# A sum of squares taken on VectorE and by products with ones, with the rotary angles moved behind it, in a two-layer hybrid transformer on one core

## The chip, the core and the metric

The kernel runs on one core of a Trainium2 chip. The metric is the device time of one execution in microseconds. The engines of the core are named as in the profile: PE (TensorE, the products), PEld (its weight loads), DVE (VectorE), ACT (ScalarE), POOL (GpSimd) and SP (SyncE, which here only issues DMAs).

## The reference

Two layers over 512 positions of width 1024, in float32. What matters here is the start of the first layer: the first norm, the rotary angles, and the first products that use both.

```python
def rmsnorm(x, g):
    xf = x.astype(jnp.float32)
    y = xf * lax.rsqrt(jnp.mean(xf * xf, axis=-1, keepdims=True) + EPS) * g.astype(jnp.float32)
    return y.astype(x.dtype)

def rope_tables(positions):
    inv_freq = ROPE_THETA ** (-jnp.arange(0, ROPE_DIM, 2, dtype=jnp.float32) / ROPE_DIM)
    ang = positions.astype(jnp.float32)[..., None] * inv_freq
    return jnp.cos(ang), jnp.sin(ang)

def reference(x, positions, ...):
    cos, sin = rope_tables(positions)
    for layer in range(DEPTH):
        h = rmsnorm(x, attn_norm[layer])
        if layer % 2 == 0:
            proj = h @ w_in_even[i]
            fq, fk, fv, ff, dq, ckv, dkr, iq, ik, iw = jnp.split(proj, split_points, axis=-1)
            ...   # forgetting attention, top-128 selected latent attention
        else:
            ...   # block attention
        x = x + conv_glu_ffn(rmsnorm(x, ffn_norm[layer]), ...)
    return rmsnorm(x, final_norm)
```

## The kernel before

x lies transposed: 8 tiles (d = 0 to 7) of 128 features by 512 positions. The norm is not applied ahead of the products. `prep` makes x times the gain, split in a high part xh (ACT, L169) and a low part xl (DVE, L170), and each product of a projection is three matmuls (L154 wh·xh, L155 wh·xl, L156 wl·xh). The factor 1/rms of each position is multiplied in later, as a row RB of 128 partitions by 512. Weights come in chunks of 128x1024 that ACT casts to a high part wh (L143; L126 for the first) and DVE or POOL turns into a low part wl (L149, L127; L147 on POOL). There are three buffers for each of raw, wh and wl, so a new chunk waits until an older one has been used.

The first layer starts with the projections misc, iq0, iq1 and ckv, 24 matmuls of 512 columns each. The norm's factor is found in `rstd_of`: the squares of the eight tiles (ACT) are added into one tile `acc`; four transposes (L187) put positions on partitions, DVE sums along the row (L189), a Newton iteration of small dependent DVE steps on 128x4 numbers (L190 to L196) gives y = 1/rms, and four more transposes (L199) spread y out as bc, which ACT copies to RB (L206). The rotary angles take a chain of some twenty small DVE steps (L285 to L305), one sine on ACT (L306, with a load of its table), and eight transposes (tabT, L321) that ACT copies to CT and ST. CR = CT·RB and SR = ST·RB (L212, L213) are what every rotated projection waits for.

The order of instructions on each engine is not the order in the source. A scheduler lays the whole program out on its own estimates and by the order of the source, then each engine runs its list strictly in order, with semaphores for what is late. So a change at the start can change places further on.

Of the kernel before, what the change touches and what calls it, by code (L numbers as in the profile page):

```python
# [18 lines left out]
F32 = mybir.dt.float32  # L19
F32R = mybir.dt.float32r  # L20
I32 = mybir.dt.int32
AF = mybir.ActivationFunctionType
OP = mybir.AluOpType
PSUM = bass.MemoryType.PSUM

P = 128
T = 512
NB = T // P
D = 1024
KT = D // P  # L30
# [41 lines left out]
def hybrid_kernel(ctx: ExitStack, tc: tile.TileContext, xT_d, pos_d, const_d, vec_d, w_d, out_d, idx):  # L72
    nc = tc.nc
    V, A, G, PE = nc.vector, nc.scalar, nc.gpsimd, nc.tensor
# [4 lines left out]
    tp = ctx.enter_context(tc.tile_pool(name="tp", bufs=1))  # L79
# [8 lines left out]
    def tmp(name):  # L88
        return tp.tile([P, T], F32, tag="tmp", name=name, bufs=N_TMP)

    def col(name, n=1):
        return tp.tile([P, n], F32, tag=f"col{n}", name=name, bufs=N_COL)

    def ps(tag, name, shape=(P, T)):
        return pp.tile(list(shape), F32, tag=tag, name=name, bufs=N_PSUM[tag])
# [5 lines left out]
    xT = cp.tile([P, KT, T], F32, name="xT")  # L101
# [5 lines left out]
    V.memset(table, 0.0)  # L107
    A.copy(table, table)
    ident = const[:, C_ID:C_ID + P]
    cmask = cp.tile([P, T], F32, name="cmask")  # L110
    G.memset(cmask[:, :384], 0.0)
    selr = cp.tile([P, P + 8], F32R, name="selr")
# [18 lines left out]
    def chunk(name, cut=0):  # L131
        raw = wp.tile([P, 1024], F32, tag="raw", bufs=N_W, name=f"raw_{name}")
        wh = wp.tile([P, 1024], F32R, tag="wh", bufs=N_W, name=f"wh_{name}")
        wl = wp.tile([P, 1024], F32R, tag="wl", bufs=N_W, name=f"wl_{name}")
        if cut:
            for s in (slice(0, cut), slice(cut, 1024)):
                nc.sync.dma_start(raw[:, s], w_d[idx[name]][:, s])
                split(wh[:, s], wl[:, s], raw[:, s])
                if s.start == 0:
                    nc.sync.dma_start(xT[:, 1], xT_d[:, 1])  # L140
            return wh, wl
        nc.sync.dma_start(raw, w_d[idx[name]])
        A.copy(wh, raw)  # L143
        if lo_on_pool:
            for n in range(0, 1024, 256):
                t = slice(n, n + 256)
                G.tensor_tensor(wl[:, t], raw[:, t], wh[:, t].bitcast(F32), op=OP.subtract)  # L147
        else:
            V.tensor_tensor(wl, raw, wh.bitcast(F32), op=OP.subtract)  # L149
        return wh, wl  # L150

    def mm3(out, ah, al, bh, bl, first, last):

        PE.matmul(out, ah, bh, start=first, stop=False)  # L154
        PE.matmul(out, ah, bl, start=False, stop=False)  # L155
        PE.matmul(out, al, bh, start=False, stop=last)  # L156

    def proj(name, w=None):
        wh, wl = w or chunk(name)
        o = ps("mm", f"mm_{name}")  # L160
        for k in range(KT):
            s = slice(k * P, k * P + P)
            mm3(o, wh[:, s], wl[:, s], xh[:, k], xl[:, k], k == 0, k == KT - 1)
        return o

    def prep(d, g, acc):

        gc = vec[:, V_G + 8 * g + d:V_G + 8 * g + d + 1]
        A.activation(xh[:, d], xT[:, d], AF.Identity, scale=gc)  # L169
        V.scalar_tensor_tensor(xl[:, d], xT[:, d], gc, xh[:, d].bitcast(F32), op0=OP.mult, op1=OP.subtract)  # L170
        if acc is not None:
            square(d, acc)

    def square(d, acc):

        if d == 0:
            A.activation(acc, xT[:, 0], AF.Square)
        else:
            s = tmp(f"sq{d}")
            A.activation(s, xT[:, d], AF.Square)  # L180
            (V if d == KT - 1 else G).tensor_tensor(acc, acc, s, op=OP.add)

    def rstd_of(acc, n, nm, nb=NB):

        st = ps("T", f"st_{nm}")[:, :nb * P]
        for b in range(nb):
            PE.transpose(st[:, b * P:b * P + P], acc[:, b * P:b * P + P], ident)  # L187
        ms, y, h, t = (col(f"{c}_{nm}", nb) for c in ("ms", "y", "h", "t"))
        V.reduce_sum(ms, st.rearrange("p (b c) -> p b c", b=nb), axis=mybir.AxisListType.X)  # L189
        V.tensor_scalar(ms, ms, 1.0 / n, EPS, op0=OP.mult, op1=OP.add)  # L190
        V.tensor_scalar(t.bitcast(I32), ms.bitcast(I32), 1, None, op0=OP.logical_shift_right)
        V.tensor_scalar(y.bitcast(I32), t.bitcast(I32), -1, 0x5F3759DF, op0=OP.mult, op1=OP.add)
        for _ in range(3):
            V.scalar_tensor_tensor(h, y, -0.5, y, op0=OP.mult, op1=OP.mult)
            V.tensor_tensor(h, h, ms, op=OP.mult)
            V.scalar_tensor_tensor(y, h, 1.5, y, op0=OP.add, op1=OP.mult)  # L196
        bc = ps("T", f"bc_{nm}")[:, :nb * P]
        for b in range(nb):
            PE.transpose(bc[:, b * P:b * P + P], y[:, b:b + 1].to_broadcast([P, P]), ident)  # L199
        return y, bc  # L200

    scale = {}

    def rstd_main(acc, nm):
        y, bc = rstd_of(acc, D, nm)
        A.copy(RB, bc)  # L206
        r = cp.tile([P, NB], F32, name=f"rstd_{nm}")
        V.tensor_copy(r, y)
        scale["col"] = r

    def rope_scaled():
        V.tensor_tensor(CR, CT, RB, op=OP.mult)  # L212
        V.tensor_tensor(SR, ST, RB, op=OP.mult)  # L213
# [12 lines left out]
    def scaled(o, nm):  # L226
        y = tmp(f"sc_{nm}")
        V.tensor_tensor(y, o, RB, op=OP.mult)
        return y
# [37 lines left out]
    def rope_angles():  # L267

        def fl(t):
            return t.rearrange("p b f -> p (b f)")  # L270

        def ang_tile(nm, k=1):
            return cp.tile([P, k * NB, 8], F32, name=f"ang_{nm}")

        def rnd(nm, src, k, c=1):
            t = ang_tile(nm, c)
            V.tensor_scalar(fl(t), fl(src), k, MAGIC, op0=OP.mult, op1=OP.add)
            V.tensor_scalar(fl(t), fl(t), -MAGIC, None, op0=OP.add)
            return t

        def fma(dst, a, k, b):
            V.scalar_tensor_tensor(fl(dst), fl(a), k, fl(b), op0=OP.mult, op1=OP.add)

        pf = cp.tile([P, NB, 1], F32, name="posf")
        V.tensor_copy(pf, pos)  # L285
        ang = ang_tile("x")
        freq = vec[:, V_FREQ:V_FREQ + 8].rearrange("p (b f) -> p b f", b=1)
        V.tensor_tensor(ang, freq.to_broadcast([P, NB, 8]), pf.to_broadcast([P, NB, 8]), op=OP.mult)

        hi = rnd("hi", ang, 1.0 / 65536.0)  # L290
        r, t = ang_tile("r"), ang_tile("t")
        fma(r, hi, -65536.0, ang)
        n0 = rnd("n0", r, 1.0 / TWO_PI)
        n2 = rnd("n2", hi, BIG / TWO_PI)
        V.tensor_scalar(fl(t), fl(hi), M2[0], None, op0=OP.mult)
        for a, k, dst in ((n0, -PI2[0], r), (n2, -PI2[0], t), (n0, -PI2[1], r), (hi, M2[1], t), (n0, -PI2[2], r),
                          (n2, -PI2[1], t), (hi, M2[2], t), (n2, -PI2[2], t)):
            fma(dst, a, k, dst)
        cs = ang_tile("cs", 2)
        V.tensor_tensor(fl(cs[:, NB:]), fl(r), fl(t), op=OP.add)  # L300
        V.tensor_scalar(fl(cs[:, :NB]), fl(cs[:, NB:]), math.pi / 2, None, op0=OP.add)
        k = rnd("k", cs, 1.0 / TWO_PI, 2)
        for p in PI2:
            fma(cs, k, -p, cs)
        V.tensor_scalar(fl(cs), fl(cs), -math.pi, math.pi, op0=OP.max, op1=OP.min)  # L305
        A.activation(fl(cs), fl(cs), AF.Sin)  # L306
        return cs
# [245 lines left out]
    def sq_acc(n):  # L553
        return cp.tile([P, T], F32, tag="acc", name=f"acc{n}", bufs=1)


    acc = sq_acc(0)
# [3 lines left out]
        nc.sync.dma_start(xT[:, d], xT_d[:, d])  # L561
    nc.gpsimd.dma_start(const, const_d)
    G.tensor_copy(cmask[:, 384:], const[:, C_TRI:C_TRI + P])
    cs = rope_angles()
    for d in range(KT):
        prep(d, 0, None)
    pmisc = proj("misc", w)
    w = [chunk("iq0")]
    acc2 = tmp("acc2")
    for d in range(KT):  # L570
        if d < 4:
            square(d, acc)
        else:
            s = acc2 if d == 4 else tmp(f"sq{d}")
            A.activation(s, xT[:, d], AF.Square)
            if d > 4:
                V.tensor_tensor(acc2, acc2, s, op=OP.add)
    V.tensor_tensor(acc, acc, acc2, op=OP.add)
    w.append(chunk("iq1"))
    V.tensor_copy(selr[0:96, :P], const[0:96, C_SEL:C_SEL + P])  # L580
    V.tensor_copy(selr[96:128, :P], const[64:96, C_SEL:C_SEL + P])
    V.tensor_scalar(selr[:, P:], const[:, C_FSEL:C_FSEL + 8], 0.5, None, op0=OP.mult)
    rope_tables(cs)
    rstd_main(acc, "n0")
    rope_scaled()

    ym = rope(pmisc, "misc")
# [41 lines left out]
    y = scaled(proj("ckv"), "ckv")  # L629
    sq = tmp("sqkv")  # L630
    A.activation(sq, y, AF.Square)
    _, bc = rstd_of(sq, P, "kv")
    yn = tmp("ckvn")
    V.scalar_tensor_tensor(yn, y, vec[:, V_GC:V_GC + 1], bc, op0=OP.mult, op1=OP.mult)
# [73 lines left out]
    for n in range(8):  # L708
        c, w = (fox if n < 4 else dsa)(n % 4)
# [13 lines left out]
    acc = sq_acc(1)  # L723
# [32 lines left out]
    for n in range(8):  # L756
        c, w = moba(n)
# [144 lines left out]
```

## Time and profile before

| | |
|---|---|
| Time, median of 3 runs | 1269.03 us (1265.8 to 1269.41) |
| The profiled execution's own time | 1267.01 us |
| Its span, first to last instruction | 1265.2 us |
| PE busy | 1221.0 us, 97% of the span |
| DVE busy | 814.5 us, 64% |
| ACT busy | 555.2 us, 44% |
| POOL busy | 359.6 us, 28% |

Busy time of PE is the time in which any matmul is in it, and matmuls overlap there; a busy PE can still run at a lower clock. What an engine waited for is named by the semaphore that came last. All times below count from the start of the span.

### The profile page before, as it was taken

The numbers are of one execution on the slowest core, as the hardware profiler recorded it, in microseconds if no ns is written. First come the engines' busy times: TensorE is split into PE (matmuls) and PEld (weight loads), VectorE is DVE, ScalarE is ACT, GpSimd is POOL, SyncE is SP. The second block draws the span as 40 slices with busy tenths as digits, with TensorE's granted clock in tenths as the row PEclk, the third lists the DMA queues.
The fourth block names the chain that finished last, engine by engine and source line by source line (L and its number), as shares of the span: only waits on it lengthen the run. The fifth ranks groups of instructions, "written<-read, shape, count | busy, mean of one in ns | idle before, by whom it ended". The sixth has DMA issues, their size and how long they took to land.

```text
span 1265.2 us, 16798 instructions
## 1 busy us (share of the span) xinstructions
PE 1221.0 (97%) x5980; PEld 1017.5 (80%) x5980; DVE 814.5 (64%) x1512; ACT 555.2 (44%) x966; POOL 359.6 (28%) x394
## 2 busy tenths in 40 slices
PE   6889999999999999999998999999999999999996
PEld 4778877777888888888887888888878888888885
DVE  7889988675555445555665778787655555544556
ACT  5564677554333332333434556556433333333234
POOL 3675556542111111111213323232212111111110
PEclk9999999999999999999999999999999999999998
DMA  5344435222333333323334434431323333333321
GB/s 193 101 113 110 114 95 138 68 82 75 94 108 94 98 101 100 95 90 97 103 100 125 112 101 117 108 106 67 97 87 100 100 101 93 92 98 101 100 84 67
DMA packets 57379, 127.24 MB, mean 101 GB/s; under 512 B 7584, under 2 KB 21024, under 8 KB 57296
## 3 DMA queue, kind: packets, MB, share of 16 engines
q1 hardware_dynamic: 56368, 124.81, 33.6%
q10 hardware_dynamic: 864, 1.17, 0.3%
q8 instruction: 47, 0.77, 0.3%
q14 instruction: 36, 0.29, 0.1%
q0 software_dynamic: 64, 0.20, 0.0%
HBM read 104.13 MB, written 2.10 MB: 84 GB/s over the span
## 4 chain that ended last, share of the span: by engine, by line
PE 79%; DVE 12%; ACT 3%; issue 3%; POOL 2%; DMA 2%; DVEq 0%; ACTq 0%; POOLq 0%; SPq 0%
PE mm_d L155 6%; PE mm_d L156 6%; PE mm_d L154 6%; PE mm_u L155 6%; PE mm_u L154 6%; PE mm_u L156 6%; PE mm_g L155 6%; PE mm_g L156 6%; PE mm_g L154 6%; DVE tmask L625 2%; DVE m L624 1%; PE t_m L367 1%; PE o_m L376 1%; PE mm_mk L154 1%; PE mm_mk L155 1%
## 5 line engine op out<-in xcount | busy, mean ns | idle before, releaser
L429 POOL TENSOR_TENSOR cv<-cv,gs 128x512 f32<-128x512 f32 x44 | 57.1, 1298 | 549.7 <-ACT gs L428 549.7
L154 PE MATMUL mm_d<-a_h,wh_d 128*128 128x512 f32 (+1 forms) x384 | 142.9, 372 | 2.2 <-ACT a_h L126 2.2
L155 PE MATMUL mm_d<-a_l,wh_d 128*128 128x512 f32 (+1 forms) x384 | 142.9, 372 | 0.5 <-DVE a_l L127 0.5
L156 PE MATMUL mm_d<-a_h,wl_d 128*128 128x512 f32 (+1 forms) x384 | 142.6, 371 | 0.0
L498 DVE TENSOR_TENSOR us<-mm_u,cv 128x512 f32<-128x512 f32 x44 | 30.4, 691 | 168.2 <-PE mm_u L156 132.7
L155 PE MATMUL mm_g<-xl,wh_g 128*128 128x512 f32 x352 | 137.2, 390 | 0.4 <-DVE xl L170 0.4
L154 PE MATMUL mm_u<-xh,wh_u 128*128 128x512 f32 x352 | 137.3, 390 | 0.0
L156 PE MATMUL mm_u<-xh,wl_u 128*128 128x512 f32 x352 | 137.0, 389 | 0.0
L155 PE MATMUL mm_u<-xl,wh_u 128*128 128x512 f32 x352 | 137.0, 389 | 0.0
L156 PE MATMUL mm_g<-xh,wl_g 128*128 128x512 f32 x352 | 136.9, 389 | 0.0
L154 PE MATMUL mm_g<-xh,wh_g 128*128 128x512 f32 x352 | 136.9, 389 | 0.0
L143 ACT CAST wh_g<-raw_g 128x1024 fp32r<-128x1024 f32 x44 | 46.3, 1053 | 155.4 <-PE mm_g L155 153.9
L495 DVE TENSOR_TENSOR gs<-mm_g,RB 128x512 f32<-128x512 f32 x44 | 30.4, 690 | 121.8 <-PE mm_g L156 119.4
L126 ACT CAST wh_d<-raw_d 128x1024 fp32r<-128x1024 f32 x45 | 47.4, 1054 | 119.3 <-PE mm_u L155 107.3
L154 PEld LDWEIGHTS mm_d<-a_h,wh_d 128*128 128x128 f32 x384 | 72.3, 188 | 15.5 <-ACT a_h L126 3.0
L155 PEld LDWEIGHTS mm_d<-a_l,wh_d 128*128 128x128 f32 x384 | 72.3, 188 | 13.5 <-DVE a_l L127 1.1
L156 PEld LDWEIGHTS mm_d<-a_h,wl_d 128*128 128x128 f32 x384 | 72.3, 188 | 12.4
L155 PEld LDWEIGHTS mm_g<-xl,wh_g 128*128 128x128 f32 x352 | 66.1, 188 | 14.8 <-DVE xl L170 1.1
L154 PEld LDWEIGHTS mm_g<-xh,wh_g 128*128 128x128 f32 x352 | 66.1, 188 | 13.8
L156 PEld LDWEIGHTS mm_u<-xh,wl_u 128*128 128x128 f32 x352 | 66.1, 188 | 13.7
L155 PEld LDWEIGHTS mm_u<-xl,wh_u 128*128 128x128 f32 x352 | 66.1, 188 | 13.6
L154 PEld LDWEIGHTS mm_u<-xh,wh_u 128*128 128x128 f32 x352 | 66.1, 188 | 13.6
(762 smaller groups left out, 3071.9 us busy)
## 6 DMA issues: line engine op xcount, KB each, us to landing
raw_g<-in_w SPq DMA_DIRECT2D x44, 512.0 KB, 3.5
raw_u<-in_w SPq DMA_DIRECT2D x44, 512.0 KB, 3.6
raw_d<-in_w SPq DMA_DIRECT2D x41, 256.0 KB, 2.9
raw_d<-in_w SPq DMA_DIRECT2D x29, 192.0 KB, 2.6
raw_d<-in_w SPq DMA_DIRECT2D x34, 128.0 KB, 2.4
raw_oe<-in_w SPq DMA_DIRECT2D x8, 512.0 KB, 4.2
raw_mv<-in_w SPq DMA_DIRECT2D x8, 512.0 KB, 3.5
raw_mk<-in_w SPq DMA_DIRECT2D x8, 512.0 KB, 4.0
```

Of the source, the lines that this page charges most:

```text
L126: A.copy(dst_h, src)
L143: A.copy(wh, raw)
L154: PE.matmul(out, ah, bh, start=first, stop=False)
L155: PE.matmul(out, ah, bl, start=False, stop=False)
L156: PE.matmul(out, al, bh, start=False, stop=last)
L367: PE.transpose(t[:, n * P:n * P + P], probs[i][:, j * P:j * P + P], ident)
L376: PE.matmul(o[:, o0:o0 + w], vj, ph[:, c0:c0 + w], start=j == 0, stop=False)
L429: G.tensor_tensor(cv, cv, gs, op=OP.mult)
L495: V.tensor_tensor(gs, og, RB, op=OP.mult)
L498: V.tensor_tensor(us, ou, cv, op=OP.mult)
L624: V.max(m8, sc)
L625: V.match_replace(sc, m8, sc, -3e38)
```

## The change

The source puts the first norm ahead of the rotary angles, and takes its sum in another way. Each tile's square is added into `acc` on DVE as soon as the tile has been prepared, for d = 1 to 6; the last square, sq7, is not added at all. In place of four transposes and a sum along the row there are eight matmuls with a 128x2 tile of ones as the moving operand: for each block of 128 positions one with `acc` and one with sq7 as the stationary operand, both into the same two columns of PSUM. A DVE copy of 128x4 numbers takes the sums out; it is held in program order. Before, three of the seven adds were on POOL and four on DVE. All of it is for the first norm; the other norms go on as before.

```diff
+    ones = tp.tile([P, 2], F32, tag="ones", name="ones")
+    V.memset(ones, 1.0)
...
-    def rstd_of(acc, n, nm, nb=NB):
+    def rstd_of(acc, n, nm, nb=NB, more=None):
...
+        if more is None:
+            for b in range(nb):
+                PE.transpose(st[:, b * P:b * P + P], acc[:, b * P:b * P + P], ident)
+            V.reduce_sum(ms, st.rearrange("p (b c) -> p b c", b=nb), axis=mybir.AxisListType.X)
+        else:
+            for b in range(nb):
+                s = slice(b * P, b * P + P)
+                PE.matmul(st[:, 2 * b:2 * b + 2], acc[:, s], ones, start=True, stop=False)
+                PE.matmul(st[:, 2 * b:2 * b + 2], more[:, s], ones, start=False, stop=True)
+            ms, st = ms.rearrange("p (b c) -> p b c", c=1), st[:, :2 * nb].rearrange("p (b c) -> p b c", c=2)
+            tc.keep_in_program_order(V.tensor_copy(ms, st[:, :, 0:1]))
+            ms = ms.rearrange("p b c -> p (b c)")
...
-    cs = rope_angles()
+    sq = None
     for d in range(KT):
         prep(d, 0, None)
+        sq = acc if d == 0 else tmp(f"sq{d}")
+        A.activation(sq, xT[:, d], AF.Square)
+        if 0 < d < KT - 1:
+            V.tensor_tensor(acc, acc, sq, op=OP.add)
     pmisc = proj("misc", w)
     w = [chunk("iq0")]
-    acc2 = tmp("acc2")
-    for d in range(KT):
-        if d < 4:
-            square(d, acc)
-        else:
-            s = acc2 if d == 4 else tmp(f"sq{d}")
-            A.activation(s, xT[:, d], AF.Square)
-            if d > 4:
-                V.tensor_tensor(acc2, acc2, s, op=OP.add)
-    V.tensor_tensor(acc, acc, acc2, op=OP.add)
+    rstd_main(acc, "n0", sq)
+    cs = rope_angles()
     w.append(chunk("iq1"))
...
     rope_tables(cs)
-    rstd_main(acc, "n0")
     rope_scaled()
```

On DVE, at the start of the program, the small angle steps (ang) stood between the low parts xl; before:

```order
L127 TENSOR_TENSOR wl_misc_104<-raw_misc_102,wh_misc_103 128x512
L277 TENSOR_SCALAR ang_n0_130<-ang_r_127 128x32
L278 TENSOR_SCALAR ang_n2_133<-ang_n2_133 128x32
L170 SCALAR_TENSOR_TENSOR xl_75<-xT_73,vec_71,xh_74 128x512
L278 TENSOR_SCALAR ang_n0_130<-ang_n0_130 128x32
L282 SCALAR_TENSOR_TENSOR ang_t_128<-ang_n2_133,ang_t_128 128x32
L581 CAST selr_83<-const_70 32x128
```

From the same instruction on, the changed kernel has:

```order
L129 TENSOR_TENSOR wl_misc_106<-raw_misc_104,wh_misc_105 128x512
L172 SCALAR_TENSOR_TENSOR xl_75<-xT_73,vec_71,xh_74 128x512
L582 TENSOR_TENSOR acc0_102<-acc0_102,sq1_127 128x512
L129 TENSOR_TENSOR wl_misc_106<-raw_misc_104,wh_misc_105 128x512
L172 SCALAR_TENSOR_TENSOR xl_75<-xT_73,vec_71,xh_74 128x512
L582 TENSOR_TENSOR acc0_102<-acc0_102,sq2_132 128x512
```

and so on, one xl and one add in turn up to the add of sq6 and the last xl; then come one angle step, the low part wl of iq0, and the copy of the sums. The rest of the angle steps stands behind that copy, in turn with the Newton steps.

On PE, at the end of the projection misc, the changed kernel has the products with ones ahead of misc's last two matmuls (st is the sum's PSUM tile; the matmuls with acc and sq7 come four times in turn):

```order
L156 MATMUL mm_misc_159<-xh_74,wh_misc_105 128x512
L197 MATMUL st_n0_190<-ones_81,acc0_102 128x2
L198 MATMUL st_n0_190<-ones_81,sq7_157 128x2
...
L156 MATMUL mm_iq0_318<-xh_74,wh_iq0_185 128x512
L157 MATMUL mm_misc_159<-xl_75,wh_misc_105 128x512
L158 MATMUL mm_misc_159<-xh_74,wl_misc_106 128x512
L157 MATMUL mm_iq0_318<-xl_75,wh_iq0_185 128x512
L156 MATMUL mm_iq1_357<-xh_74,wh_iq1_261 128x512
L157 MATMUL mm_iq1_357<-xl_75,wh_iq1_261 128x512
L158 MATMUL mm_iq0_318<-xh_74,wl_iq0_186 128x512
```

Before, misc's last matmuls were followed at once by those of iq0, and the four transposes of the sum stood 26 matmuls further on, behind the eight of the rotary tables; now bc comes first and the tables behind it.

Further on, in the first layer's attention, the lists differ in many small places until the output projection; from there on they are the same. One of these places on DVE, about 95 to 99 us into the profile of before, has the selection of the largest scores (MAX, MATCH_REPLACE on tmask), a new query (sc_fq, fq_l) and the split of transposed probabilities (pt). Before:

```order
L228 TENSOR_TENSOR sc_fq1_930<-mm_fq1_905,RB_84 128x512
L625 MATCH_REPLACE tmask2_90<-m8_2_1482,tmask2_90 128x384
L624 MAX m8_2_1485<-tmask2_90 128x8
L127 TENSOR_TENSOR fq1_l_933<-sc_fq1_930,fq1_h_932 128x512
L127 TENSOR_TENSOR pt_f00_0l_942<-t_f00_0_945,pt_f00_0h_941 128x512
```

And now:

```order
L240 TENSOR_TENSOR sc_fq1_935<-mm_fq1_910,RB_86 128x512
L631 MAX m8_2_1490<-tmask2_92 128x8
L632 MATCH_REPLACE tmask2_92<-m8_2_1490,tmask2_92 128x384
L129 TENSOR_TENSOR fq1_l_938<-sc_fq1_935,fq1_h_937 128x512
L631 MAX m8_2_1493<-tmask2_92 128x8
L632 MATCH_REPLACE tmask2_92<-m8_2_1493,tmask2_92 128x384
L631 MAX m8_2_1496<-tmask2_92 128x8
L129 TENSOR_TENSOR pt_f00_0l_947<-t_f00_0_950,pt_f00_0h_946 128x512
```

Three steps of the selection have come between fq_l and pt.

## Rows read from the trace of the kernel before

**Rows 1.** Stretches: us, busy time (count) by engine, granted clock, DMA share, GB/s.
```profile
0.00:20.00 20.00, 9.44 (x24) 6.43 (x25) 14.26 (x40) 13.66 (x22) 7.84 (x16) 1.00 0.65 226
20.00:45.00 25.00, 22.62 (x107) 18.19 (x106) 21.78 (x48) 9.45 (x13) 11.20 (x13) 0.93 0.36 105
45.00:160.00 115.00, 107.17 (x603) 90.53 (x603) 104.72 (x278) 67.24 (x141) 69.85 (x90) 0.99 0.42 113
```

**Rows 2.** Waits of PE, 0 to 330 us: total us, times, longest.
```profile
PE mm_misc L155 <- DVE xl L170: 3.5, 1, 3.5
PE bc_n L199 <- DVE y_n L196: 2.2, 1, 2.2
PE t_f L367 <- DVE pt_f_0l L127: 1.9, 4, 1.3
```

**Rows 3.** Timeline, 7 to 21 us: start, us, engine, line, instruction.
```profile
7.51 0.68 DVE L127 TENSOR_TENSOR wl_misc<-raw_misc,wh_misc 128x512 fp32r<-128x512 f32 x1
8.19 3.54 POOL L181 TENSOR_TENSOR acc<-acc,sq 128x512 f32<-128x512 f32 x2 [0.81 <-ACT sq L180]
9.03 1.31 DVE L282 SCALAR_TENSOR_TENSOR ang_t<-ang_n,ang_t 128x32 f32<-128x32 f32 x1
10.62 1.64 DVE L127 TENSOR_TENSOR wl_misc<-raw_misc,wh_misc 128x512 fp32r<-128x512 f32 x1
13.49 0.74 DVE L170 SCALAR_TENSOR_TENSOR xl<-xT,vec,xh 128x512 fp32r<-128x512 f32 x1
14.54 0.18 DVE L282 SCALAR_TENSOR_TENSOR ang_t<-ang_hi,ang_t 128x32 f32<-128x32 f32 x1
17.68 0.74 DVE L170 SCALAR_TENSOR_TENSOR xl<-xT,vec,xh 128x512 fp32r<-128x512 f32 x1
18.44 0.68 DVE L577 TENSOR_TENSOR acc<-acc,sq 128x512 f32<-128x512 f32 x1
19.43 1.22 DVE L149 TENSOR_TENSOR wl_iq<-raw_iq,wh_iq 128x1024 fp32r<-128x1024 f32 x1
20.71 0.51 PE L156 MATMUL mm_iq<-xh,wl_iq 128*128 128x512 f32 x1
```

**Rows 4.** The chain that ended last, 15 to 28 us: start, us, what.
```profile
16.36 0.43 PE mm_misc L156
22.59 0.23 PE mm_iq L154
26.43 0.67 PE st_n L187 x4
```

**Rows 5.** Timeline, 21 to 44 us.
```profile
21.25 1.28 ACT L306 ACT_TABLE_LOAD   x1
25.15 1.03 PE L321 MATMUL tabT<-const,exp_tab 128*128 128x128 f32 x8
27.12 0.69 DVE L189 TENSOR_REDUCE ms_n<-st_n 128x4 f32<-128x512 f32 x1 [0.84 <-PE st_n L187]
27.39 1.05 ACT L143 CAST wh_fv<-raw_fv 128x1024 fp32r<-128x1024 f32 x1 [0.53 <-ACT ST L322]
28.46 0.16 DVE L194 SCALAR_TENSOR_TENSOR h_n<-y_n 128x4 f32<-128x4 f32 x1
32.27 1.09 PE L199 MATMUL bc_n<-const,y_n 128*128 128x128 f32 x4 [2.23 <-DVE y_n L196]
34.02 0.69 DVE L212 TENSOR_TENSOR CR<-CT,RB 128x512 f32<-128x512 f32 x1 [1.68 <-ACT RB L206]
36.78 1.77 DVE L223 TENSOR_TENSOR ry_misc<-ry_misc,rs_misc 128x512 f32<-128x512 f32 x1 [0.20 <-POOL rs_misc L222]
43.28 0.39 PE L156 MATMUL mm_ckv<-xh,wl_ckv 128*128 128x512 f32 x1
```

**Rows 6.** One stretch of 1 us, columns as in the first group.
```profile
33.00:34.00 1.00, 1.00 (x4) 0.82 (x3) 0.00 (x0) 0.58 (x1) 0.00 (x0) 0.50 0.84 336
```

**Rows 7.** DVE's timeline, 96 to 98 us.
```profile
96.98 0.56 DVE L624 MAX8 m<-tmask 128x8 f32<-128x384 f32 x1
```

More of the change, by code (lines that the diff above doesn't have):

```diff
@@ L181, in square @@
             (V if d == KT - 1 else G).tensor_tensor(acc, acc, s, op=OP.add)
-    def rstd_of(acc, n, nm, nb=NB):
+    def rstd_of(acc, n, nm, nb=NB, more=None):
         st = ps("T", f"st_{nm}")[:, :nb * P]
-        for b in range(nb):
-            PE.transpose(st[:, b * P:b * P + P], acc[:, b * P:b * P + P], ident)
         ms, y, h, t = (col(f"{c}_{nm}", nb) for c in ("ms", "y", "h", "t"))
-        V.reduce_sum(ms, st.rearrange("p (b c) -> p b c", b=nb), axis=mybir.AxisListType.X)
+        if more is None:
[10 more added lines that the diff above has]
+            ms = ms.rearrange("p b c -> p (b c)")
         V.tensor_scalar(ms, ms, 1.0 / n, EPS, op0=OP.mult, op1=OP.add)
@@ L202, in hybrid_kernel, with rstd_main @@
     scale = {}
-    def rstd_main(acc, nm):
-        y, bc = rstd_of(acc, D, nm)
+    def rstd_main(acc, nm, more=None):
+        y, bc = rstd_of(acc, D, nm, more=more)
         A.copy(RB, bc)
```

## The prediction, made before the changed kernel was run

> **What bounds the kernel now.** I read the busy times by stretch first, then the waits of PE, then the timelines of the first 45 us, then the chain for the spacing of PE's products, and at last DVE in the attention. PE holds 107.2 of 115 us from 45 to 160 us, but 9.4 of 20 and 22.6 of 25 us before that [rows 1]. So the start is where PE stands still, and there are two large holes in it that the change touches. PE waits 3.5 us for a low part xl, and 2.2 us for the y of the first norm ahead of the transposes bc [rows 2]. Behind the second hole the clock is low: the granted clock is 0.50 in the stretch from 33 us on [rows 6], which is 1.2 GHz. Products of 512 columns follow each other at 0.43 us at 16 us and at 0.23 us at 22 us [rows 4]; the first is the pace of the low clock, the second that of 2.4 GHz.
>
> The first hole is made by DVE and POOL together. While POOL adds two squares, from 8.19 us for 3.54 us, an angle step on DVE takes 1.31 us, where a like one takes 0.18 us later; the low part of misc takes 1.64 us, where its other half took 0.68 us [rows 3]. The second hole is the Newton chain, whose steps start late, behind the sum at 27.12 us, and end in bc at 32.27 us [rows 5].
>
> From 45 to 160 us DVE is busy 104.7 of 115 us [rows 1], so a lead that only one of PE and DVE has won would be waited away there. I therefore follow both to the end of ckv: PE's last ckv product starts at 43.28 us, and DVE's CR, from which its dense stretch begins, at 34.02 us [rows 5].
>
> **The change part by part.** *Adds on DVE, none on POOL, no angle steps between.* From the low part at 7.51 us on [rows 3] DVE has seven low parts xl, six adds, and the second half of misc's low part, in one row. An xl takes 0.74 us and an add 0.68 us [rows 3]; in a dense row they overlap by some 0.07 us (the 0.74 us xl at 17.68 is followed by an add at 18.44 [rows 3], with a small step between), so I count 0.72, 0.65 and 0.63. From 8.12 us: one xl, one add and the half chunk to 10.1; then five pairs of xl and add, 6.9 us, to 17.0; the last xl to 17.7. That is 0.7 us ahead of the end at 18.42 us before (17.68 + 0.74 [rows 3]). The stall of 3.5 us disappears, and six adds of 0.65 us, 3.9 us in all, take its place: the tiles now come one every 1.37 us, where three products at the low clock take 1.28. ACT keeps pace, one high part and one square per tile. The adds that go from POOL free it for 4.8 us (3.54 + 1.26, of which the first is shown [rows 3]), when it has nothing else to do. The ones are written once, under the wait for the first tile: nothing. No DMA is added, and the first weight buffer is free earlier, so SP's queue is not held longer.
>
> *The products with ones.* They need the add of sq6 (17.0 us) and stand on PE behind tile 6, which ends at about 17.7 us at the low clock. No row shows a float32 matmul that isn't a transpose. From below: eight at the pace of the table transposes, 1.03 us for eight [rows 5], are 1.0 us. From above: eight at the low pace of a 512-column product, 0.43 us [rows 4], are 3.4 us. The nearest row is a transpose at the low clock, since its weights are float32 too and 128x128: four of bc took 1.09 us [rows 5], less their common tail some 0.22 us each, so 1.8 us. I take that: st ends at 19.5 us.
>
> The Trainium skill (FP8 and Floating Point Precision, TensorE Precision Notes) says that true float32 makes four passes through the array. By that page eight products would cost four times the lowest bound, an estimate of 4.1 us, and st would end at 21.8 us; a transpose's row can't show it. Without these sentences the range stands as it is.
>
> *From there to ckv on PE.* Six products follow, two of them iq1's, at 0.23 us (1.4 us), so the third product of iq0 starts at 20.9 us; before it started at 20.71 [rows 3], with none of iq1 done. PE is level there. On DVE the low part of iq0 ends at about 19.1 us; the copy of the sums then heads DVE's list and waits 0.4 us for st. Queued behind it are the other low parts (iq1, ckv) and all angle steps. Thirty-two rows lie between that copy and the last y: two 128x1024 low parts of 1.22 us [rows 3], a shuffle of 0.7 us, and the small steps, in two chains in turn, at 0.1 us each, half the 0.2 us that a dependent step takes alone (0.16 us [rows 5] and a gap). That is 6.2 us, so y is there at 25.7 us. PE by then has 24 products to do from 20.9 us, 5.5 us, to 26.4 us. The hole of 2.2 us is gone, and with it the low clock behind it: seven products at 0.43 instead of 0.23 and a slower bc, 1.7 us.
>
> What is late next: the rotary tables. ACT has the cast of wh_fv ahead of the sine; it needs iq0's weight buffer, free at about 25.6 us, takes 1.05 us, and the table load 1.28 us [rows 5] comes behind. The sine and half of the copies, taken as four small steps, make 0.7 us. So tabT starts at 28.7 us; PE, after bc (0.5 us) and four products, stands there from 27.8 us: a new wait of 0.9 us. With the 1.03 us of tabT and 16 products (3.7 us) iq1 ends at 33.4 us. Next the four transposes of misc now stand ahead of ckv instead of inside it. They wait for the rotated misc: CR can start at 30.0 us (first tabT half at 29.3, a copy on ACT 0.6 us), then SR, product and shuffle to 32.7 us, then the sum, which took 1.77 us beside POOL [rows 5]: 34.5 us, a wait of 1.1 us, where before it was about 0.5 us. The transposes take 0.5 us and 24 products 5.5 us: ckv's last product starts at 40.3 us. That is 3.0 us ahead of 43.28. DVE's CR is 4.0 us ahead.
>
> *The sum.* PE at ckv: hole and low clock gone, 2.2 + 1.7; other savings (bc at the high clock, the old st of 0.67 us [rows 4], two iq1 products ahead) 1.3; less 0.2 for the later start, 0.9 at the tables, 0.6 at misc's transposes and some 0.5 of lost overlap: 3.0 us. DVE has 4.0. Both engines lead, so neither waits the other's lead away, and from the output projection on the lists are the same. I take 3.2 us, nearer to PE. The span goes from 1265.2 to 1262.0 us, and the profiled execution from 1267.0 to 1263.8; the median of the runs lies 2.0 us above that execution, so 1265.8 us.
>
> **The rivals.** *More is won (1262.5 us).* If the products with ones cost the lower bound (0.8 us less) and the two leads are both kept in full by reordering at the tables, 4.0 + 0.8 = 4.8 us, and up to 1.5 more in the attention, where PE waits 1.9 us in four places for a split that comes earlier by the DVE lead [rows 2]. Taken together 6.5 us. Against it: the table load and the sum beside POOL are in the way.
>
> *Nothing is won: the low clock stays (1269 us).* Tiles come every 1.37 us for 9 us. If PE's clock has risen meanwhile, its three products take 0.69 us and it stands idle half of each 1.37. Before, the products still followed each other at 0.43 us at 16 us, behind the first hole, and at 0.23 us at 22 us [rows 4]; the second hole, of 2.2 us [rows 2], was enough for the fall [rows 6]. If the gaps bring the clock down, or the products with ones keep it down, the first 16 products or so behind them run at 0.43: 16 x 0.20 = 3.2 us, the whole lead. For it: the first stretch starts low anyway, and short gaps are new. Against it: no gap is longer than 0.7 us. The Trainium skill (TensorE: Matmul & The Clock Gate, A second HAM failure mode: psum-queue depth-cycling) tells of a kernel in which small idle times between groups of matmuls made the clock go up and down; by that page this rival would be the likelier one, but no row here shows a fall after gaps so short.
>
> *Slower: the attention's new order (1273 us).* The selection now puts three steps between fq_l and the split pt. Each takes 0.56 us or more [rows 7], so the split comes 1.8 us later against its neighbours. PE waits for that split in four places now, 1.9 us in all [rows 2]. If in each the 1.8 us come on top, 7.2 - 3.2 = 4.0 us are lost: 1273.0. It decides where PE has no products between the transposes and what needs the split; for it speaks that DVE has few gaps there [rows 1], against it that the steps are only moved, not added, and that the scheduler has moved products of fv ahead of that place too.
>
> **How the numbers follow.** The runs of before lie 3.6 us apart, 0.28%; so a difference of under 0.3%, 3.8 us, can't be told from none here. The forecast, a gain of 1.5 to 5 us (1264 to 1267.5), has 0.50; the gain above 3.8 us in it about 0.26, below 0.24. More won 0.14, all of it faster. The low clock 0.20, all the same. The attention's order 0.16, of which 0.13 slower and 0.03 within. So faster 0.40, same 0.47, slower 0.13. The range goes to 1260.5 below (the larger gain, with 2 us for the runs) and to 1271.5 above, which takes in the low clock, the costly products with ones (1.6 us more, and DVE behind them as late) and part of the attention's loss.
>
> **What would show it.** Right: no wait of PE for an xl over 1 us, xl and adds on DVE in turn to 17.7 us, angle steps of 0.18 us, no wait of over 0.5 us before bc, the granted clock at 1.00 from 32 to 36 us, a wait before tabT and one before misc's transposes of about 1 us each, CR at 30 us, ckv's last product at 40.3. Wrong: eight products with ones in over 3.4 us, with DVE idle before the copy of the sums; products at 0.43 us behind 19 us; waits for pt over 4 us in all; or a lead at 45 us that is gone at 160 us.

## The result, and the profile after

| | before | changed |
|---|---|---|
| Time, median of 4 runs each, on one chip | 1267.41 us (1264.9 to 1269.41) | 1276.98 us (1275.75 to 1278.88) |
| Ratio, with its 95% interval | | 1.0085 (1.0069 to 1.0100) |
| Span of the profiled execution | 1265.2 us | 1274.5 us |

The change makes the kernel 0.85% slower; the prediction was a gain of 0.25%. The start went nearly as forecast. Timeline of the changed kernel, 14 to 30 us:

```profile
14.35 0.68 DVE L582 TENSOR_TENSOR acc<-acc,sq 128x512 f32<-128x512 f32 x1
14.95 0.74 DVE L172 SCALAR_TENSOR_TENSOR xl<-xT,vec,xh 128x512 fp32r<-128x512 f32 x1
16.22 0.73 DVE L172 SCALAR_TENSOR_TENSOR xl<-xT,vec,xh 128x512 fp32r<-128x512 f32 x1
...
16.54 0.28 PE L197 MATMUL st_n<-ones,acc 128*128 128x2 f32 x2
18.02 0.36 PE L198 MATMUL st_n<-ones,sq 128*128 128x2 f32 x2
18.42 0.16 DVE L200 COPY ms_n<-st_n 128x4 f32<-128x4 f32 x1 [0.25 <-PE st_n L198]
...
24.25 0.16 DVE L208 SCALAR_TENSOR_TENSOR y_n<-h_n,y_n 128x4 f32<-128x4 f32 x1
24.70 1.05 ACT L145 CAST wh_fv<-raw_fv 128x1024 fp32r<-128x1024 f32 x1 [4.65 <-DVE rstd_n L220]
25.18 0.60 PE L211 MATMUL bc_n<-const,y_n 128*128 128x128 f32 x4
25.76 1.28 ACT L318 ACT_TABLE_LOAD   x1
27.06 0.26 ACT L318 ACTIVATE ang_cs<-ang_cs 128x64 f32<-128x64 f32 x1
28.90 1.06 PE L333 MATMUL tabT<-const,exp_tab 128*128 128x128 f32 x8 [2.19 <-DVE exp_tab L330]
```

Low parts and adds stand in turn, the last xl is there 1.5 us earlier than [rows 3] had it, the sum is out at 18.4 us where the row sum started at 27.12 [rows 5], and bc waits for nothing where it waited 2.2 us [rows 2]. But PE now waits 2.2 us at the tables. In this execution the clock falls behind that hole, as it fell behind the old one [rows 6]; one stretch of 1 us of the changed kernel, granted clock third from the right:

```profile
31.00:32.00 1.00, 1.00 (x4) 0.77 (x3) 1.00 (x4) 0.00 (x0) 0.45 (x1) 0.50 0.45 180
```

The loss lies behind the start. Stretches of before, and then of the changed kernel, with columns as in [rows 1]:

```profile
100.00:152.00 52.00, 50.45 (x295) 43.36 (x294) 49.82 (x133) 26.64 (x63) 27.41 (x39) 1.00 0.38 102
152.00:222.00 70.00, 67.28 (x373) 55.19 (x372) 58.22 (x158) 49.76 (x125) 42.51 (x59) 1.00 0.47 119
222.00:340.00 118.00, 115.97 (x534) 93.64 (x533) 73.38 (x123) 55.75 (x93) 45.67 (x48) 1.00 0.26 81
```
```profile
100.00:152.00 52.00, 49.30 (x284) 42.31 (x283) 48.14 (x131) 28.62 (x67) 26.91 (x39) 1.00 0.36 98
152.00:222.00 70.00, 59.68 (x315) 48.50 (x314) 50.68 (x131) 41.11 (x104) 37.68 (x53) 0.95 0.40 102
222.00:340.00 118.00, 115.57 (x540) 93.06 (x539) 76.70 (x138) 59.00 (x107) 48.78 (x54) 1.00 0.27 79
```

From 152 to 222 us PE has 315 products in its records instead of 373, and a mean clock of 0.95; from 222 us on the two are alike. The waits of PE from 100 to 225 us (total us, times, longest), of before and then of the changed kernel:

```profile
PE mm_dq L154 <- DVE dv L127: 1.8, 1, 1.8
PE t_f L367 <- DVE pt_f_0l L127: 1.7, 3, 1.3
PE s_d L263 <- DMA dq_a<-dq_l: 0.6, 1, 0.6
```
```profile
PE mm_dq L156 <- DVE dv L129: 4.7, 2, 2.9
PE s_f L275 <- DMA fq_a<-fq_h: 3.0, 2, 1.7
PE t_f L379 <- DVE pt_f_0l L129: 1.9, 2, 1.2
PE s_d L275 <- DMA dq_a<-dq_l: 1.3, 1, 1.3
PE o_d L388 <- ACT pt_d_0h L128: 1.0, 1, 1.0
PE s_f L275 <- DMA fq_l<-fq_h: 0.8, 1, 0.8
PE t_d L379 <- DVE pt_d_0l L129: 0.4, 1, 0.4
```

That is 13.1 us against 4.1. The 9 us more, and the full-speed time that a clock of 0.95 leaves out of 70 us (3.5 us), come to 12.5 us; this estimate is near the loss of 12 us in the table below. The wait for the split pt_f, of which my third rival spoke, grew by 0.2 us.

How far a kernel is ahead is read by taking the start of the same instruction in its profile and in that of before. Lead (minus) or lag, us; the experiments of the last three columns are told below:

| instruction (its time before) | changed | new start, old order | sine first, old order | sine first, new order |
|---|---|---|---|---|
| DVE CR (34.0) | -3.8 | -4.1 | -4.9 | -6.0 |
| PE st_kv (46.4) | -1.2 | -1.0 | -4.4 | -2.2 |
| PE mm_fk, first half (111.9) | -0.9 | -0.2 | -3.9 | +0.1 |
| PE mm_dq (153.0) | -1.3 | -0.2 | -4.0 | -0.3 |
| PE mm_dq (175.6) | +3.9 | +0.1 | -3.7 | +3.6 |
| PE s_d (205.4) | +9.5 | +0.1 | -3.7 | +9.3 |
| PE o_d (252.5) | +10.5 | +0.1 | -3.7 | +10.2 |

Two things are to be explained: the lead of 3.8 us at CR is down to 1.2 at 46 us, and 12 us are lost between 153 and 222 us, where no source line was changed.

### The profile page after: what moved, and what is told of

It is laid out like the page before. It is cut to its first block, busy times and chain, and to the rows that moved or that the text cites. A ratio compares the mean times of both kernels' runs of the same rounds, so it can differ in the third digit from the quotient of the medians.

```text
span 1274.5 us, 16810 instructions
## 1 busy us (share of the span) xinstructions
PE 1222.4 (96%) x5992; PEld 1018.1 (80%) x5992; DVE 812.4 (64%) x1515; ACT 555.0 (44%) x966; POOL 353.0 (28%) x391
## 4 chain that ended last, share of the span: by engine, by line
PE 73%; DVE 5%; ACT 3%; issue 2%; DMA 2%; POOL 2%; SPq 0%; ACTq 0%; DVEq 0%; POOLq 0%
PE mm_d L157 6%; PE mm_d L158 6%; PE mm_d L156 6%; PE mm_u L157 6%; PE mm_u L156 6%; PE mm_u L158 6%; PE mm_g L157 6%; PE mm_g L158 6%; PE mm_g L156 6%; DMA mq_l<-mq_h 1%; PE t_m L379 1%; PE o_m L388 1%; PE mm_mk L157 1%; PE mm_mk L158 1%; PE mm_mk L156 1%
## 5 line engine op out<-in xcount | busy, mean ns | idle before, releaser
L128 ACT CAST wh_d<-raw_d 128x1024 fp32r<-128x1024 f32 x45 | 47.4, 1054 | 119.3 <-PE mm_u L157 107.3
```

Source lines behind the costliest of these rows:

```text
L128: A.copy(dst_h, src)
```

## The experiments

**How an order is held.** What both kernels trace from `rope_scaled()` on is the same instructions in the same order of the source. The scheduler's lists differ in it only up to some 260 us (PE's first 1054 places, DVE's 309, ACT's 193, POOL's 127, SP's 100). So the lists of either kernel can be laid on the other by edges that fix the issue order on an engine and wait for nothing:

```diff
+    body = len(nc.cur_bb.bb.instructions)
     rope_scaled()
...
+    traced = list(nc.cur_bb.bb.instructions)[body:]
+    order_only = mybir.DependencyInfo(mybir.DependencyClass.NoSync, mybir.DependencyReason.DATA)
+    for line in _orders():
+        for p, q in zip(line, line[1:]):
+            tc.add_manual_dep(traced[q], traced[p].name, order_only, reason="order")
```

`_orders()` gives one list of places for each engine. In the experiments below only these lists change, if nothing else is said. Ratios are to the kernel before, run on the same chip.

**Start or order?** *new_start_old_order*: the changed source with the lists of before. *old_start_new_order*: the source of before with the lists of the change.

> The changed kernel, with one thing put back: behind the start, every engine's list up to some 260 us is held in the order of the kernel before. Theory A (the start wins what it was meant to win, and the new order of the attention loses it and more): the lead at CR (3.8 us in the changed kernel) is kept, and the time is 1264 us (1262 to 1266.5), 3 to 4 us under the kernel before. Rival B (the start's own operations, or when they end, make the attention slower, whatever its order): 1275 to 1278 us, as the changed kernel. Rival C (half and half): 1267 to 1272.

> The kernel before, start and all, with the lists behind the start held in the order of the changed kernel. Theory A: it loses the 13 us that the changed kernel loses between CR and 260 us, with no lead to set against it: 1280 us (1276 to 1285). Rival B: as before, 1266 to 1269. Rival C: 1270 to 1275.

1265.03 us, ratio 0.9984 (0.9969 to 1.0000), and 1279.92 us, ratio 1.0120 (1.0105 to 1.0136). The order alone makes before 15 us slower; without it the change wins 0.16%, some 2 us, with an interval from 0 to 4. So Theory A holds for the loss and rival B falls; of A's gain of 3 to 4 us about half is there. In the table the lead of new_start_old_order is gone by 112 us, but that is one execution: it took 1267.9 us, the longest of eleven with a median of 1265.0 and a minimum of 1259.2. What it lost is told under the start below.

**Which engine's list?** *weights_new_pe_dve_old* takes PE's and DVE's lists from before and the three others from the change; *pool_old* takes POOL's alone from before.

> The changed kernel with PE's and DVE's lists in the order of before, and ACT's, POOL's and SP's (the casts and low parts of the weights, their DMAs, the copies and exponentials) as the change has them. Theory A1 (the later casts of the weights wh_ukv, wh_dq on ACT cost it, since PE and DVE then wait for the weights): 1274 to 1279 us. Theory A2 (PE's and DVE's own order costs it): 1263 to 1267.

> The changed kernel with POOL's list alone in the order of before, the others as the change has them. If POOL's order (low parts wl_ukv and wl_dq behind the scalings prt and the low parts o_f_l) costs the loss: 1264 to 1269 us. If it is ACT's order, PE's or DVE's: 1275 to 1279, since the low parts then still wait for late casts.

1292.47 us, ratio 1.0225 (1.0210 to 1.0240), and 1276.88 us, ratio 1.0092 (1.0079 to 1.0106). With late weights and PE and DVE in the old order the loss more than doubles, so A2 falls: putting PE's and DVE's lists back does not bring the time back. Their order in the change reads as an answer to the late casts. The opposite run, PE and DVE as the change has them and the other three as before, was not made, so what those two lists cost by themselves is open. A1 has the sign, at a price far over mine. POOL's list alone, put back, changes nothing that can be told (1.0092 against 1.0085).

**Which stretch?** The lists can be cut where both have issued the same instructions. All three have the change's start; *new_order_to_105*, *new_order_105_152* and *new_order_from_152* have the change's lists in that stretch alone, *act_dq3_late* in eleven places on ACT alone (from the cast wh_dq3 to the copies p behind it).

```diff
 ACT CAST dk_h<-mm_dk (second pair)
-ACT CAST wh_dq<-raw_dq (fourth chunk)
 ACT CAST p<-t_f
 ACT ACTIVATE prt_d,sm_d<-prt_d,mx_d
...
+ACT CAST wh_dq<-raw_dq (fourth chunk)
 ACT CAST p<-t_f
```

> The changed kernel's start, with the lists in the change's order up to about 105 us and in the order of before from there on. In the trace of the changed kernel PE still leads by 0.9 us at 112 us and by 1.3 at 153 us, so the loss should lie behind: 1264 to 1266 us. If the loss is made ahead of 105 us (where the reordered selection stands between fq_l and the split pt, the mechanism of my third rival) and only shows later: 1270 us or more.

> The changed kernel's start, with the change's order only from about 105 to 152 us (there the cast wh_ukv stands six places later on ACT, wh_dq1 six places), and the order of before ahead of it and behind. By the leads in the trace (no loss between 112 and 153 us): 1264 to 1267 us. If late weights are what costs, and what is late is set here: 1268 to 1272.

> The changed kernel's start, with the order of before up to about 152 us and the change's order only behind it (there the cast wh_dq3 stands ten places later on ACT, and PE has its dq products and the scores of the latent heads in another order). By the leads (the changed kernel goes from 1.3 us ahead at 153 us to 10.5 us behind at 222): 1273 to 1278 us. If the loss needs what goes ahead of it: 1264 to 1268.

> The changed kernel's start and the order of before everywhere, but for eleven places on ACT: the cast wh_dq3 comes ten places later, behind the exponentials prt_d and the casts pt_f and p, as the change has it; the other ten follow in the change's order. If this late cast is what costs the stretch behind 152 us (PE waits for wl_dq3, which POOL makes from it): 1268 to 1274 us. If the order of PE's own products costs it: 1264 to 1266.

1266.67 us, ratio 1.0004 (0.9991 to 1.0018); 1273.20, 1.0061 (1.0040 to 1.0081); 1272.22, 1.0050 (1.0031 to 1.0069); 1270.26, 1.0030 (1.0016 to 1.0044). These four have the change's start, so they are to be set against new_start_old_order (0.9984): on it the order up to 105 us costs 0.2%, at the edge of what can be told, the two later stretches 0.8 and 0.7%, and the whole order 1.0% (1.0085 over 0.9984), which is less than its parts together. The leads had pointed to the last stretch alone. By itself the middle one lags by 4.4 us at 153 us and 9.9 at 162, which it does not inside the whole new list: neighbouring stretches are made for each other. The waits of PE in new_order_105_152, 100 to 152 and then from 152 us, name what is late:

```profile
PE o_f L436 <- ACT pt_f_0h L176: 2.0, 1, 2.0
PE t_f L427 <- DVE pt_f_0l L177: 1.4, 1, 1.4
PE s_f L323 <- DMA fq_l<-fq_h: 0.6, 1, 0.6
...
PE s_f L323 <- DMA fq_a<-fq_h: 3.6, 1, 3.6
```

The late cast wh_dq3, with the ten places around it, costs 0.5% on this start, some 6 us and more than half of what its stretch does. Its profile, of its shortest run (1264.4 us), is 4.9 us ahead at mm_dq (175.6) and 1.9 us behind at s_d (205.4). The longest wait of PE in between:

```profile
PE t_d L427 <- POOL prt_d L408: 4.4, 1, 4.4
```

The changed kernel has no such wait. ACT casts wh_dq3 at 179.4 us here, and POOL, in the order of before, has its low part ahead of prt_d; the change's list has prt_d (187.0 us) ahead of that low part (189.0 us). So this run shows what one late cast can cost in the lists of before, and not what it costs in the changed kernel.

**Is it one place?** In the changed kernel the longest stall runs through four engines (timeline, 201 to 208 us); then the same steps in before, where PE does not wait for them:

```profile
201.56 2.83 POOL L149 TENSOR_TENSOR wl_oe<-raw_oe,wh_oe 128x256 fp32r<-128x256 f32 x4 [4.30 <-ACT wh_oe L145]
204.34 1.26 POOL L234 TENSOR_TENSOR rs_dq<-rs_dq,SR 128x512 f32<-128x512 f32 x1
205.64 0.85 DVE L235 TENSOR_TENSOR ry_dq<-ry_dq,rs_dq 128x512 f32<-128x512 f32 x1 [2.64 <-POOL rs_dq L234]
206.41 1.27 DVE L129 TENSOR_TENSOR dv<-mm_dv,dv 128x512 fp32r<-128x512 f32 x2
207.15 0.65 PE L156 MATMUL mm_dq<-xh,wh_dq 128*128 128x512 f32 x1 [2.90 <-DVE dv L129]
```
```profile
193.71 2.83 POOL L147 TENSOR_TENSOR wl_oe<-raw_oe,wh_oe 128x256 fp32r<-128x256 f32 x4 [1.53 <-ACT wh_oe L143]
196.49 1.29 POOL L222 TENSOR_TENSOR rs_dq<-rs_dq,SR 128x512 f32<-128x512 f32 x1
197.56 0.68 DVE L127 TENSOR_TENSOR dv<-mm_dv,dv 128x512 fp32r<-128x512 f32 x1
198.16 0.68 DVE L223 TENSOR_TENSOR ry_dq<-ry_dq,rs_dq 128x512 f32<-128x512 f32 x1
198.72 0.39 PE L154 MATMUL mm_dq<-xh,wh_dq 128*128 128x512 f32 x1
```

ACT casts wh_oe later; POOL stands 4.3 us for it with rs_dq queued behind; DVE stands for rs_dq with dv queued behind; PE stands for dv. Three runs, each the changed kernel, take such places apart. *dv_first* moves dv ahead on DVE, *q_copies_first* two copies ahead of a weight load on SP, *three_moves* does both and puts rs_dq ahead on POOL:

```diff
+DVE TENSOR_TENSOR dv<-mm_dv,dv (first half)
+DVE TENSOR_TENSOR ry_dq<-ry_dq,rs_dq
 DVE RECIPROCAL sm_d<-sm_d
-DVE TENSOR_TENSOR ry_dq<-ry_dq,rs_dq
-DVE TENSOR_TENSOR dv<-mm_dv,dv (first half)
...
+SP DMA fq_a<-fq_h
+SP DMA fq_a<-fq_l
 SP DMA raw_oe<-in_w
-SP DMA fq_a<-fq_h
-SP DMA fq_a<-fq_l
...
+POOL TENSOR_TENSOR rs_dq<-rs_dq,SR
 POOL TENSOR_TENSOR wl_oe<-raw_oe,wh_oe x4
-POOL TENSOR_TENSOR rs_dq<-rs_dq,SR
```

> The changed kernel with three DVE instructions near 202 us in the order of before: the low part dv of the latent values' first half ahead of ry_dq and of the reciprocal sm_d, instead of behind them. In the changed kernel DVE stands 2.6 us before ry_dq for POOL's product rs_dq, and PE 2.9 us before mm_dq for dv, with the clock at 0.73 in the 5 us around it. If this one place in DVE's list makes that stall: the wait of PE goes below 0.5 us, and the time falls by 3 to 5 us from the changed kernel's 1277, to 1272 to 1274. If PE then only waits for the next thing (dq_l of the same product): 1275 to 1278.

> The changed kernel with two DMA issues on SP moved: the copies of fq_h and fq_l into fq_a (fourth pair of heads) ahead of the load of the weights raw_oe, which near 154 us waits 7.0 us for POOL's wl_dq. In the changed kernel fq_h is cast by 151.3 us and its copy is issued at 154.6; PE then waits 1.7 us for it. If the load ahead of the copies is what holds them: the copies are issued at 152 and 153.6 us, PE's wait goes, and the time falls by 1.5 to 3 us, to 1274 to 1275.5. If the copies aren't what PE waits for in effect (DVE's split pt, or the later places): 1276 to 1278.

> The changed kernel with both moves of the two runs before, dv kept ahead of the reciprocal alone, and on POOL the product rs_dq (third pair of latent heads) ahead of the four low parts of wl_oe, which wait 4.3 us for ACT's cast. If the loss behind 150 us is these queues (a ready step behind one that waits for late weights): 5 to 8 us of the changed kernel's loss come back, 1269 to 1272 us. If the loss is spread over many places: 1274 to 1277.

1276.48 us, ratio 1.0081 (1.0067 to 1.0095); 1278.30, 1.0096 (1.0082 to 1.0110); 1274.59, 1.0071 (1.0058 to 1.0083). The two single moves do nothing that can be told. The three together win some 2 us of 10, and even that is not clear of the noise (1.0058 to 1.0083 against 1.0069 to 1.0100). Waits of PE in dv_first from 152 to 225 us:

```profile
PE o_d L436 <- ACT pt_d_0h L176: 3.4, 2, 2.4
PE mm_dq L204 <- DVE dv L177: 1.8, 1, 1.8
```

The wait for dv fell from 4.7 to 1.8 us as meant, and PE stands 2.4 us more for ACT's cast pt_d instead. In q_copies_first the wait for fq_a behind 152 us is gone too, and the time is not better. So taking away the stalls shown brings little or nothing back; they look like places where something late comes to light. That the late casts of weights are the cause in the changed kernel is argued from the traces and not shown by a run.

**What holds the start back?** *sine_first* has the change's source, the lists of before, and one edge more: ACT's cast wh_fv (24.70 us above) stands behind the sine.

```diff
-        A.activation(fl(cs), fl(cs), AF.Sin)
+        sine.append(A.activation(fl(cs), fl(cs), AF.Sin))
...
+    tc.add_manual_dep(traced[154], sine[0].ins.name, order_only, reason="order")
```

> The changed kernel's start with the order of before behind it, and one more edge at the start: ACT's cast wh_fv stands behind the sine instead of ahead of it. In the changed kernel the cast, 1.05 us from 24.7, and the table load behind it hold the sine until 27.1 us, although its angles are there at 25.1; PE waits 2.2 us before tabT and runs at 0.50 from 30 to 33 us. With the edge tabT starts by 26.8 us and PE does not wait there over 0.5 us. If a lead of the start is kept: 2 to 4 us under the run with the order of before alone (1265.0), 1261 to 1263. If the lead is waited away between 36 and 100 us: 1264 to 1266, with a lead at CR of some 6 us that is below 2 us at 98 us.

1258.55 us (1256.8 to 1261.99), ratio 0.9941 (0.9927 to 0.9955): better than both kernels, and the best of all that ran; the profile is of its longest run, 1261.99. Its timeline, 20 to 41 us:

```profile
20.37 1.28 ACT L368 ACT_TABLE_LOAD   x1
25.29 0.26 ACT L368 ACTIVATE ang_cs<-ang_cs 128x64 f32<-128x64 f32 x1 [3.64 <-DVE ang_cs L367]
26.07 1.05 ACT L193 CAST wh_fv<-raw_fv 128x1024 fp32r<-128x1024 f32 x1 [0.52 <-PE mm_iq L205]
27.86 0.60 PE L383 MATMUL tabT<-const,exp_tab 128*128 128x128 f32 x4
28.98 0.60 PE L383 MATMUL tabT<-const,exp_tab 128*128 128x128 f32 x4
...
32.87 1.05 ACT L193 CAST wh_fv<-raw_fv 128x1024 fp32r<-128x1024 f32 x1 [2.66 <-PE mm_iq L205]
...
40.59 0.68 DVE L288 TENSOR_TENSOR sc_ckv<-mm_ckv,RB 128x512 f32<-128x512 f32 x1
```

The table load is done while ACT waits for the angles, PE has no wait before tabT, and the clock stays up from there on. The scheduler, which lays the start out anew, has also put three products between the halves of tabT, so the edge moved more than the cast. In the profile of new_start_old_order the hole at tabT and the low clock held up iq1's products; ACT's next cast wh_fv, which waits for their buffer, came at 35.28 us instead of 32.87:

```profile
35.28 1.06 ACT L193 CAST wh_fv<-raw_fv 128x1024 fp32r<-128x1024 f32 x1 [4.89 <-issue]
36.24 0.61 ACT L176 CAST ik_h<-ry_misc 64x512 fp32r<-64x512 f32 x1
36.41 4.17 POOL L197 TENSOR_TENSOR wl_fv<-raw_fv,wh_fv 128x256 fp32r<-128x256 f32 x4 [2.55 <-ACT wh_fv L193]
36.88 0.80 DVE L177 TENSOR_TENSOR ik_l<-ry_misc,ik_h 64x512 fp32r<-64x512 f32 x1 [0.67 <-ACT ik_h L176]
40.61 2.25 DVE L177 TENSOR_TENSOR iq_l<-ry_iq,iq_h 128x512 fp32r<-128x512 f32 x1
```

ik_h stood behind it, DVE waited for ik_h, and POOL's low parts then ran beside DVE's, whose 0.68 us steps took up to 2.25. That is the lead of 4.1 us that was 1.0 at 46 us. In sine_first 4.4 us are left there and 3.7 at 252 us.

The low clock has the larger part in this. act_dq3_late has the same lists as new_start_old_order up to some 170 us and the same hole of 2.2 us ahead of tabT, but in its profile the clock did not fall:

```profile
26.00:36.00 10.00, 7.80 (x42) 6.43 (x41) 7.79 (x18) 4.74 (x9) 6.12 (x8) 1.00 0.23 79
```

There the lead is 3.8 us at st_kv and 5.2 us at mm_dq (153.0), against 1.0 and 0.2 us. So with the lists of before and without the sine's edge the lead depends on whether the clock falls behind the hole, which it does in some executions only. The change's lists lose it even so: new_order_to_105 has no fall ahead of 44 us, and its lead is 4.1 us at CR and 1.6 us at st_kv, where PE waits 2.7 us for ACT's sqkv.

**Which part of the change?** *sum_only_old_order* has the new sum, with the angles ahead of the norm as before; *norm_first_old_order* has the sums of before, with the norm ahead of the angles; both hold the lists of before. *sum_only* is the first with no order held, *sine_free* is the changed kernel with the sine's edge alone and no order held.

```diff
+    cs = rope_angles()
     sq = None
...
-    rstd_main(acc, "n0", sq)
-    cs = rope_angles()
...
     rope_tables(cs)
+    rstd_main(acc, "n0", sq)
     rope_scaled()
```

(for sum_only and sum_only_old_order, against the changed source; for norm_first_old_order, against the source of before:)

```diff
-    cs = rope_angles()
     for d in range(KT):
...
     V.tensor_tensor(acc, acc, acc2, op=OP.add)
+    rstd_main(acc, "n0")
+    cs = rope_angles()
...
     rope_tables(cs)
-    rstd_main(acc, "n0")
```

> The new sum alone (adds on DVE as the tiles come, eight products with ones), with the rotary angles and tables ahead of the norm as before, and the order of before held behind the start. Here ACT has the sine and both table copies ahead of the cast wh_fv, so nothing holds the tables. If the sum wins the start: CR 4 to 6 us earlier than before and kept, 1259 to 1262 us. If putting the norm ahead of the angles was what won: 1264 to 1267.

> The other part alone: the sums as before (three adds on POOL, four on DVE, transposes and a row sum), the norm put ahead of the angles, the order of before held behind the start. The wait for xl (3.5 us) should stay, with DVE's angle steps and POOL's adds in it; ACT has wh_fv ahead of the sine again, as in the changed kernel. If the norm's place wins nothing or loses by the held-up sine: 1266 to 1270 us. If it wins: 1260 to 1264.

> The new sum alone, angles ahead of the norm as before, and no order held: the scheduler lays out the attention, and by its lists it chooses the change's order but for a few places. If the order costs by itself: 1270 to 1275 us, about 11 more than the same start with the order of before. If the order costs only where the start has lost its lead: 1260 to 1265.

> The changed kernel as it is, no order held, with the one edge that puts ACT's cast wh_fv behind the sine; the scheduler keeps the change's order but for a few places. If the order's loss adds to whatever the start wins: 1258.6 + 11 to 13, 1270 to 1272 us. If the loss came from the lost lead: 1259 to 1264.

1263.20 us, ratio 0.9976 (0.9965 to 0.9987); 1266.47, 0.9997 (0.9988 to 1.0006); 1281.05, 1.0108 (1.0094 to 1.0123); 1275.94, 1.0069 (1.0057 to 1.0081). The sum alone wins 3 us, the norm's place alone nothing, and both with the sine in its place 7.5. sum_only_old_order missed its range by 1 us. The order costs some 16 to 18 us on top of either good start (1281.05 against 1263.20, 1275.94 against 1258.55), over the 11 to 13 expected. By the lists it is the sum that brings the new order about: the lists of sum_only are the change's but for a few places, and norm_first without held lists would have those of before but for a few.

## Why the prediction was wrong

The step that failed is the sentence that closes the sum: "Both engines lead, so neither waits the other's lead away, and from the output projection on the lists are the same." That the lists agree from there on is true, and the loss is made ahead of it. Between ckv and the output projection I priced the scheduler's new lists at nothing; they cost some 13 us (1.0%) with the change's start and 15 (1.2%) with the start of before.

The rival that named the order had the right sign, but neither the place nor the mechanism. The reordering it named, steps of the selection ahead of the split pt, lies ahead of 105 us, and the order up to there costs 0.2%. It counted the split pt, 7.2 us on top of 1.9; PE's waits for it came to 2.7 us in all (0.8 ahead of 100 us, 1.9 behind). What grew in the trace are the waits for dv, the query's copies and pt_d, at the end of a queue: behind 105 us eight casts of weights stand one to ten places later on ACT, POOL's low parts wait for them, and what stands behind them on POOL, SP and DVE waits too. That the lists cost this time is shown; that the late casts are what makes them cost it stays argued. Such casts are off PE's chain in the profile of before, and I priced only steps that PE waited for there.

The second step that failed is the term "0.9 at the tables". tabT came at 28.90 us (forecast 28.7), but PE was there 1.1 us earlier than I had it (26.7 for 27.8), so the wait was 2.2; and I had taken the clock as saved, where in the profiled execution it fell again behind the new hole. sine_first shows what this was worth: 0.9984 against 0.9941, some 5.4 us.

Right were: the wait for xl (largest 0.3 us), the products with ones (1.8 us, from the transposes' row), bc without a wait, CR at 30.2 us (forecast 30.0), ckv's last product at 40.7 (40.3), so PE's lead of 2.6 us (3.0) and DVE's of 3.8 (4.0) where I followed them to. I stopped there; at st_kv, PE's next step, 1.2 us of it were left. The 0.6 at misc's transposes was not paid in the profile of the changed kernel, whose iq1 came late by the low clock; the five profiles with the same lists there and no fall ahead of them (dv_first, q_copies_first, three_moves, pool_old, new_order_to_105) have that wait with 1.2 us, for the 1.1 of the forecast. For the products the Trainium skill (FP8 and Floating Point Precision, TensorE Precision Notes) led to an estimate of 4.1 us; the measured 1.8 us decides.

The low-clock rival was wrong for the changed kernel: its gaps of 0.3 us brought no fall. Its price was 16 products at 0.43 us: most falls in the profiles last 3 to 4 us, some seven to nine products, and two (in old_start_new_order from 13 us and in pool_old from 82 us) last 6.8 us, which is 16. One reading of the prediction stays open: products came at 0.43 us up to 16 us, but the granted clock of 0 to 20 us stands at 1.00 [rows 1], so the granted clock does not account for the slow pace there. The sign of the third rival was right and its chance, 0.13, too small.

## What to carry to other kernels

A change at the start of a program that a scheduler lays out is two changes: the work, and a new list on every engine. Hold the old list behind the change and time both, before judging the work. Look in the new lists for loads and casts of weights that moved back, on the engines that PE never waits for; their price can show later and elsewhere, and moving the step that shows it may only move the stall. Take more than one execution into account before a lead in one trace is called kept or lost. And when a wait goes, ask at once who arrives early at the next one.

## What the runs showed of the hardware

A float32 product with two moving columns (two records in the profile) took 0.36 us, one after the other at 0.22 us, its 128x128 weights among it (16.54 to 18.02 above); the transposes bc took 0.60 us for four at that clock.

The clock after a hole is not the same in every execution. In before a wait of 2.2 us at 30 us and one of 2.6 at 81 us were each followed by 3 to 4 us at 0.50; in the changed kernel the same wait of 2.6 us was not. Eleven profiles have the change's start with its wait of 2.2 to 2.3 us ahead of tabT: in five the clock fell behind it (the changed kernel, new_start_old_order, weights_new_pe_dve_old, new_order_105_152, new_order_from_152), in the other six it did not.

In sine_first it fell at 18.9 us, behind three waits of 0.3 us for xl and the products with ones; that execution lost some 1.7 us by it (an estimate: 3.4 us at 0.50). The Trainium skill (TensorE: Matmul & The Clock Gate, A second HAM failure mode: psum-queue depth-cycling) tells of a kernel in which small idle times between groups of matmuls made the clock go up and down. But new_order_to_105 and q_copies_first have four such waits and the same products, and no fall there, so these runs do not show that such gaps bring the clock down, as my second rival had it.

Over the 12 runs of new_order_to_105 (1264.1 to 1271.9 us) the time goes with the mean granted clock (correlation -0.91, 1.3 us for each 0.001). As 0.001 of such a run is 1.3 us, the spread is about what the lost clock would make; which falls made it was not counted.
